# Sums of weight blocks of the two Gates and of two token-row projections on VectorE in place of POOL

## The chip, the cores and the metric

The kernel runs on one core of one Trainium2 chip. The time is that of one launch on the device, in microseconds (us). The core's engines are TensorE (PE: matmuls; PEld: the loading of their stationary operand, which goes beside them), VectorE (DVE), ScalarE (ACT), GpSimd (POOL) and SyncE (SP), on whose queue the kernel's DMAs are issued. Each engine runs its own instructions in the order of the program and waits on semaphores for the others. All data is float32.

## The reference

One layer of a backbone over 1024 latent tokens of width 1024, with 256 context tokens:

```python
def ffn_sublayer(h, shift, scale, gate, g, w_in, w_out):      # w_in 1024 x 5632, w_out 2816 x 1024
    hn = modulate(rmsnorm(h, g), shift, scale)
    a, b = jnp.split(hn @ w_in, 2, axis=-1)
    y = (jax.nn.silu(a) * b) @ w_out
    return h + 0.5 * gate[:, None, :] * y

h  = ffn_sublayer(h, mods[0], mods[1], mods[2], g_ffn1, w_ffn1_in, w_ffn1_out)
hc = ffn_sublayer(hc, mods_c[0], mods_c[1], mods_c[2], g_ffn1, w_ffn1_in, w_ffn1_out)
p_lat = project(h, mods[3], mods[4], g_mix, w_in, PROJ_SIZES)
p_ctx = project(hc, mods_c[3], mods_c[4], g_mix, w_in, ctx_sizes)
...
y_lat = merge_branches(p_lat[4:], hlf + hlb, g_head, g_sgu, w_s, b_s, w_branch_a, w_branch_b, w_out)
h = h + mods[5][:, None, :] * y_lat
h = ffn_sublayer(h, mods[6], mods[7], mods[8], g_ffn2, w_ffn2_in, w_ffn2_out)
return rmsnorm(h, g_final)
```

In place of the dots stand a bidirectional mLSTM over chunks of 128 tokens, fed with q, k, v and gates out of the projection, and a spatial gating unit, fed with two more parts of it (u and vs). `mods` are nine vectors, silu(c) @ w_ada + b_ada.

## The kernel before, in words

**Products.** Every float32 product is made as three matmuls of a rounded type: each operand is split into a high part (a ScalarE cast, L143) and a low part (a VectorE subtraction, L144), and high x high, high x low and low x high are added up in PSUM. L143 and L144 are those two lines of the helper `split`; its results are called `ring` (weights), `fa`, `fb`, `fc`, `mx` (activations) or `fhl` (results that go on to the next product).

**Seven in place of eight.** The big products are cut into 2 x 2 blocks and made with seven block products in place of eight (`p` = 1 to 7). For this, sums and differences of the blocks of the weights are needed, each an operation over 128 x 512 numbers, and sums of the activations (`Factors`, L292), made once. What this case is about is which engine makes the sums of the weights.

**Gate** is the first half of an FFN on the latent tokens: A (Gate 1, weights `w1i`) and B (Gate 2, `w2i`). A has 22 feature blocks f. Each takes seven steps, one for a p, of 12 matmuls with 512 columns (L389), in the order 1, 2, 5, 6, 7, 4, 3 for the first three blocks, the heads, whose steps go side by side, and then woven block by block with the last two steps of a block among the next one's (`self.steps`). Steps 1, 6, 7 and 4 add into one PSUM bank (`qa`), 5 and 3 into a second and 2 into a third (both `qb`). ScalarE copies the result of step 1 (L404) out of the bank before step 6 may write into it, then that of 6 (L410) and 5 (L413); VectorE adds the result of 2 (L406) and 7 (L415), multiplies with that of 4 (L417), adds that of 3 (L420) and multiplies the two halves (L422), after ScalarE's silu (L407, L421). L438 makes sums of the finished blocks for the next product.

`Gate.load` takes a step's weights, splits them into a page of the ring and is called by `fill`, as soon as a page is free. A block has two raw pages of 128 x 1024 (`half`, loaded from L348: a1 a2 and b1 b2, in tiles `rawq`, or `rawh` for the heads). `presum` makes s1 = b1 + b2 (L355) and b1 = a1 - b1 (L356); step 6 makes a1 = s1 - a1 (L371); step 3 makes a2 = a2 - a1 (L373). Four per block, two Gates: 176 sums. The heads' pages are loaded ahead by `preload`, with their presum: for A in the loop of the context's FFN (L921), for B in `fin_o`, while the product with w_o runs. The ring has 4 pages, and 3 (A) or 5 (B) more once the space for them is free.

**Rows** (L1117) makes the projections to v (`wv`) and vs (`wvs`) with the tokens as rows. It too has seven products; its sums are at L1140, L1142, L1144 and L1146, four times each in each projection: 32. `Stream.fill` calls `load` four entries ahead or more. **Pair** makes the other projections; its sums (L1203 to L1207) are on VectorE in both kernels.

**Order.** A scheduler puts the instructions of each engine in order by the dependences of the program as it is written, and each engine then runs them strictly in that order. Beside the Gate of stage A the adaLN vectors are made in the background: `tick` runs a step of them after each step of the Gate (VectorE L749 and L751 over pages `adapg`, 144 loads of 256 KB). Other side work lies in the list `todo`, from which `pump` takes some after each group of matmuls. `Norm` makes the statistics of a norm (TensorE L201, VectorE L210, TensorE L214 `rb`) and writes the normed activations.

Of the kernel before, what the change touches and what calls it, by code (L numbers as in the profile page):

```python
# [13 lines left out]
ALU = mybir.AluOpType  # L14
# [34 lines left out]
def build(tc, a, out):  # L49
    nc = tc.nc  # L50
    ctx = ExitStack()
    with ctx:
        _build(ctx, tc, nc, a, out)


def _build(ctx, tc, nc, a, out):
    V, S, G, T = nc.vector, nc.scalar, nc.gpsimd, nc.tensor
# [38 lines left out]
    def t2(name, dt=F32, shape=(128, 512)):  # L96
        return tp.tile(list(shape), dt, name=name, tag="t2", bufs=12)

    def mm_ps(name):
        return ps.tile([128, 512], F32, name=name, tag="mm", bufs=4)  # L100
# [4 lines left out]
    class Weights:  # L105
# [10 lines left out]
        def load(self):  # L116
            n, i, w = self.order.popleft()
            src = a[n][i]
            if self.n % 4 < 2:
                raw = self.pool.tile([128, w], F32, name="raw", tag="raw", bufs=2)  # L120
            else:
                raw = hnp.tile([128, w], F32, name="raw", tag="pg1", bufs=8)
            self.n += 1
            nc.sync.dma_start(raw, src)
            hl = self.pool.tile([128, 2, w], F32R, name="hl", tag="hl", bufs=3)
            split(hl, raw)
            self.ready.append((n, i, hl))
            self.held += 1
# [13 lines left out]
    def split(hl, src):  # L142
        S.copy(hl[:, 0, :], src)  # L143
        V.tensor_sub(hl[:, 1, :], src, hl[:, 0, :].bitcast(F32))  # L144
# [31 lines left out]
    def proj(pt, wl, pgs, first):  # L176
        mm3(pt, [wk(wl, k) + (pgs[k][:, 0, :], pgs[k][:, 1, :]) for k in range(NKT)], first)
# [138 lines left out]
    class Gate:  # L316
# [31 lines left out]
                nc.sync.dma_start(s[i], a[self.name][2 * f + i])  # L348
            return s[i][:, 0:512], s[i][:, 512:1024]

        def presum(self, f):
            a1, a2 = self.half(f, 0)
            b1, b2 = self.half(f, 1)
            s1 = self.s[f]["s1"] = self.sums("s1")
            G.tensor_tensor(s1, b1, b2, ALU.add)  # L355
            G.tensor_tensor(b1, a1, b1, ALU.subtract)  # L356

        def load(self):
            f, p = key = self.order.popleft()
            if p in (1, 2):  # L360
                src = self.half(f, 0)[p - 1]
                self.half(f, 1)
            else:
                a1, a2 = self.half(f, 0)
                b1, b2 = self.half(f, 1)
                s = self.s[f]

                if p in (5, 6) and "s1" not in s:
                    self.presum(f)
                if p == 6:  # L370
                    G.tensor_tensor(a1, s["s1"], a1, ALU.subtract)  # L371
                elif p == 3:
                    G.tensor_tensor(a2, a2, a1, ALU.subtract)  # L373
                src = {6: a1, 5: s["s1"], 7: b1, 4: b2, 3: a2}[p]
            hl = self.ring()
            split(hl, src)
            self.ready.append((key, hl))
            self.held += 1
            if p == 3:
                del self.s[f]  # L380
# [178 lines left out]
    class Stage:  # L559
# [15 lines left out]
                          lambda n: s1v.popleft(), NFP, HEAD)  # L575
            self.heads = [(f, i) for i in (0, 1) for f in self.q.head]

        def preload(self):
            if self.heads:
                f, i = self.heads.pop(0)  # L580
                self.q.half(f, i)
                if i:
                    self.q.presum(f)

        def rpage(self, name, shape=(128, 2, 512), dt=F32R):
            return self.rg.tile(list(shape), dt, name=name, tag="ring2", bufs=self.ring2)
# [256 lines left out]
    A = Stage("1", "w1i", 3)  # L843
# [53 lines left out]
    def slow(fn, *args, cost=1024):  # L897
        f = it(fn, *args)
        f.cost = cost
        todo.append(f)  # L900

    for f in range(NF):
        if f < NKT:
            for tb in range(2):
                nc.sync.dma_start(h[tb][f], a["xT"][f, :, tb * 512:(tb + 1) * 512])
        if 2 <= f < 2 + NKT:
            for tb in range(2):
                slow(add_pos, tb, f - 2)
                slow(n1[tb].sq, f - 2)
                slow(nc.sync.dma_start, hsp[tb, f - 2], h[tb][f - 2], cost=0)  # L910
        if f == 2 + NKT:
            todo.extend([n1[0].rstd, nop, n1[1].rstd, nop, n1[0].bcast, n1[1].bcast])
            for d in range(NKT):
                slow(n1[0].inplace, d, s0, b0)
                slow(A.F.early, fpage, 1 if d < 4 else 2, d % 4)
            for d in range(NKT):
                slow(n1[1].inplace, d, s0, b0)
        if f == 12:
            A.head()
        if f > 12:  # L920
            A.preload()  # L921
        wa = W.take("w1i", 2 * f)
        wb = W.take("w1i", 2 * f + 1)
        if f % 2 == 0:
            pa, pb = mm_ps("pa"), mm_ps("pb")
        for pt, w_ in ((pa, wa), (pb, wb)):
            proj(pt[:, f % 2 * 256:f % 2 * 256 + 256], w_, hnc, f % 2 == 0)
            W.done()
        if f % 2 == 0:
            continue  # L930
        sil = t2("sil")
        S.activation(sil, pa, AF.Silu)
        V.tensor_mul(sil, sil, pb)
        g = [t2("gc", F32R) for _ in range(2)]
        S.copy(g[0], sil)
        V.tensor_sub(g[1], sil, g[0].bitcast(F32))
        for y in range(2):
            nc.sync.dma_start(gcsp[f // 2, y].rearrange("p f c -> p (f c)"), g[y].bitcast(F32))
# [125 lines left out]
    class Stream:  # L1064
# [13 lines left out]
        def fill(self):  # L1078
            while self.q and len(self.ready) < 4 + self.extra:
                if isinstance(self.q[0], Bar):  # L1080
                    if not self.q[0].up:
                        return
                    self.q.popleft()
                    continue
                load, run = self.q.popleft()
                src = load()
                hl = self.ring()
                split(hl, src)
                self.ready.append((run, hl))
# [27 lines left out]
    class Rows:  # L1117
# [13 lines left out]
        def load(self, p, k):  # L1131
            if p in (1, 2):
                i = k if p == 1 else k + 4
                if i not in self.r:
                    self.get(i, rawpg if p == 1 else raw2)
                return self.r[i][:, 0:512]
            a1, b1 = self.r[k][:, 0:512], self.r[k][:, 512:1024]
            a2, b2 = self.r[k + 4][:, 0:512], self.r[k + 4][:, 512:1024]
            if p == 7:
                G.tensor_tensor(b1, a1, b1, ALU.subtract)  # L1140
            elif p == 6:
                G.tensor_tensor(b2, b2, b1, ALU.subtract)  # L1142
            elif p == 5:
                G.tensor_tensor(a1, a1, b2, ALU.add)  # L1144
            elif p == 3:
                G.tensor_tensor(a2, a2, b2, ALU.subtract)  # L1146
            return {7: b1, 4: b2, 6: b2, 5: a1, 3: a2}[p]

        def prod(self, p, k, hl):
# [112 lines left out]
    def rows_steps(name, emit, side=(), early=False):  # L1262
        r = Rows(name, emit, early)
        n = 0
        for p in RSEQ:
            for k in range(4):
                st.q.append((lambda p=p, k=k: r.load(p, k), lambda hl, p=p, k=k: r.prod(p, k, hl)))
                n += 1
                if n == 4:
                    st.q.append(r.bar)  # L1270
            if p == 2:
                for load, run in side:
                    st.q.append((lambda load=load: load(r), run))
                    n += 1
        return n, r.bar
# [818 lines left out]
```

## Time and profile before

Three runs took 2684.61, 2685.7 and 2685.88 us; the profiled execution took 2682.41 us, with a span of 2680.3 us and a mean granted TensorE clock of 0.997. Its busy times by stage, in us, all from windows of the trace (the moved sums of POOL are in the stages named in bold):

| us from the start | stage | length | PE | DVE | ACT | POOL |
|---|---|---|---|---|---|---|
| 0 to 178 | adaLN, context FFN in | 178 | 171.72 | 132.28 | 97.86 | 12.35 |
| 178 to 603 | **Gate 1** | 425 | 421.46 | 324.88 | 179.38 | 129.82 |
| 603 to 880 | FFN 1 out | 277 | 276.47 | 231.01 | 135.71 | 0.00 |
| 880 to 1060 | **rows of wv**, gates | 180 | 179.18 | 104.10 | 80.72 | 26.93 |
| 1060 to 1380 | projections to q, k, o and more | 320 | 320.00 | 231.42 | 164.71 | 0.00 |
| 1380 to 1560 | **rows of wvs**, context states | 180 | 180.00 | 117.53 | 71.03 | 22.84 |
| 1560 to 1920 | mLSTM heads, w_b | 360 | 357.95 | 247.95 | 85.00 | 115.61 |
| 1920 to 2022 | w_a to w_o, **heads of Gate 2** | 102 | 100.91 | 72.52 | 51.01 | 14.02 |
| 2022 to 2452 | **Gate 2** | 430 | 424.00 | 307.28 | 189.24 | 114.80 |
| 2452 to 2680 | FFN 2 out, final norm | 228 | 218.47 | 147.77 | 87.08 | 4.21 |

How to read the profile: a row of instructions starts with its place in time, or with the line of the kernel; "out<-in" names the tiles; "x24" counts instructions. A wait in square brackets is the engine's idle time ahead of the row and what ended it. In the list of waits, a row is the waiting engine and line, what it waited for, and then the us in total, the number of waits and the longest. An engine's busy time counts overlapping records once. Records of instructions in a row overlap by some 0.08 us, so that two of 0.69 us appear as one row of some 1.3 us.

### The profile page before, as it was taken

Reading aid. Unit: us, or ns where it says so; the run is one execution under the profiler, and the core shown is the slowest. Engines: PE = TensorE matmul, PEld = TensorE weight load, DVE = VectorE, ACT = ScalarE, POOL = GpSimd, SP = SyncE. Lnnn points to the kernel's source line nnn. Section 1 sums busy time; section 2 is a strip of 40 time slices with the busy share of each in tenths; the row PEclk is TensorE's granted clock in tenths of the full one; section 3 lists DMA queues with packets and bytes.
Section 4 is the critical chain, followed back from the end, with each engine's and each line's share of the span. In section 5 each row is a group of like instructions: output and inputs, shape, how many; then the busy total and the mean of one; then the engine's idle time right before and its main releaser. Section 6 shows DMA issues by size and latency. Waiting matters only on the chain.

```text
span 2680.3 us, 35678 instructions
## 1 busy us (share of the span) xinstructions
PE 2650.2 (99%) x12754; PEld 2210.3 (82%) x12754; DVE 1916.7 (72%) x3243; ACT 1141.7 (43%) x1952; POOL 440.6 (16%) x422
## 2 busy tenths in 40 slices
PE   9999999999999999999999999999999999999998
PEld 5998888888889878888888888888887788888887
DVE  4897688686979646687664868677568766675855
ACT  4664444344336525564443443121245444344432
POOL 0041333220000210000002005342102323230000
PEclk9999999999999999999999999999999999999999
DMA  8842344369578222356553467448140332337645
GB/s 299 315 173 99 142 165 149 114 217 327 156 254 281 85 79 86 106 169 199 194 176 105 140 238 268 166 167 279 58 159 24 126 140 99 135 122 274 201 157 173
DMA packets 202240, 456.73 MB, mean 170 GB/s; under 512 B 20432, under 2 KB 54480, under 8 KB 202064
## 3 DMA queue, kind: packets, MB, share of 16 engines
q1 hardware_dynamic: 202064, 454.47, 49.6%
q8 instruction: 100, 1.64, 0.3%
q14 instruction: 76, 0.62, 0.1%
HBM read 328.95 MB, written 125.51 MB: 170 GB/s over the span
## 4 chain that ended last, share of the span: by engine, by line
PE 89%; DVE 6%; issue 2%; DMA 1%; ACT 1%; SPq 0%; POOL 0%; POOLq 0%; ACTq 0%; DVEq 0%
PE pq L1240 17%; PE qa L389 17%; PE po L508 14%; PE qb L389 12%; PE pt L1719 9%; PE pr L1159 6%; PE pc L1030 2%; PE pn L1832 2%; PE pu L1559 2%; PE pa L169 1%; PE pb L169 1%; PE pkc L1219 1%; PE adr L811 1%; PE pn L1830 1%; DVE h L292 1%
## 5 line engine op out<-in xcount | busy, mean ns | idle before, releaser
L144 DVE TENSOR_TENSOR ring<-rawq,ring 128x512 fp32r<-128x512 f32 x408 | 310.6, 762 | 204.9 <-ACT ring L143 202.2
L508 PE MATMUL po<-gring,wring 128*128 128x512 f32 (+1 forms) x1896 | 425.1, 385 | 0.5 <-DMA gring<-fsp 0.5
L508 PEld LDWEIGHTS po<-gring,wring 128*128 128x128 f32 x1896 | 349.5, 188 | 71.9 <-issue 1.0
L143 ACT CAST ring<-rawq 128x512 fp32r<-128x512 f32 x408 | 252.9, 621 | 299.5 <-PE pq L1240 82.1
L389 PE MATMUL qa<-fc,ring 128*128 128x512 f32 x1056 | 252.6, 390 | 2.3 <-DVE ring L144 1.4
L389 PEld LDWEIGHTS qa<-fc,ring 128*128 128x128 f32 x1056 | 198.1, 188 | 44.2 <-DVE ring L144 1.8
L1240 PE MATMUL pq<-fc,ring 128*128 128x512 f32 x864 | 207.8, 393 | 0.0
L143 ACT CAST wring<-rw 128x512 fp32r<-128x512 f32 x154 | 95.9, 622 | 228.3 <-PE po L508 220.9
L1240 PEld LDWEIGHTS pq<-fc,ring 128*128 128x128 f32 x864 | 161.6, 188 | 33.3
L1719 PE MATMUL pt<-yp,ring 128*128 128x512 f32 x768 | 183.9, 396 | 1.2 <-ACT ug L1297 1.2
L144 DVE TENSOR_TENSOR wring<-rw,wring 128x512 fp32r<-128x512 f32 x154 | 106.3, 691 | 93.9 <-ACT wring L143 93.7
L1719 PEld LDWEIGHTS pt<-yp,ring 128*128 128x128 f32 x768 | 144.2, 188 | 30.7 <-ACT ug L1297 1.4
L1240 PE MATMUL pq<-fa,ring 128*128 128x512 f32 x576 | 142.3, 395 | 0.0
L1240 PE MATMUL pq<-fb,ring 128*128 128x512 f32 x576 | 138.2, 394 | 0.0
L389 PE MATMUL qa<-fb,ring 128*128 128x512 f32 x528 | 128.6, 394 | 3.7 <-ACT p L404 3.7
L389 PE MATMUL qa<-fa,ring 128*128 128x512 f32 x528 | 127.7, 391 | 1.2 <-DVE ring L144 0.7
L389 PE MATMUL qb<-fb,ring 128*128 128x512 f32 x528 | 126.8, 390 | 1.2 <-DVE p L406 0.6
L1240 PEld LDWEIGHTS pq<-fb,ring 128*128 128x128 f32 x576 | 107.7, 188 | 23.7 <-issue 0.2
L389 PE MATMUL qb<-fa,ring 128*128 128x512 f32 x528 | 126.2, 389 | 0.0
L389 PE MATMUL qb<-fc,ring 128*128 128x512 f32 x528 | 126.2, 389 | 0.0
L751 DVE SCALAR_TENSOR_TENSOR adacc<-adapg,sc,adacc 128x512 f32<-128x512 f32 x140 | 111.4, 814 | 20.1 <-DMA adapg<-in_w_ada_dram 19.3
L1240 PEld LDWEIGHTS pq<-fa,ring 128*128 128x128 f32 x576 | 106.9, 188 | 22.5 <-DVE ring L144 0.2
(342 smaller groups left out, 4803.9 us busy)
## 6 DMA issues: line engine op xcount, KB each, us to landing
adapg<-in_w_ada_dram SPq DMA_DIRECT2D x144, 256.0 KB, 3.7
fsp<-fhl SPq DMA_DIRECT2D x66, 512.0 KB, 2.6
gring<-fsp SPq DMA_DIRECT2D x66, 512.0 KB, 4.2
raw<-in_w1i_dram SPq DMA_DIRECT2D x44, 512.0 KB, 5.5
graw<-fsp SPq DMA_DIRECT2D x88, 256.0 KB, 3.6
rawq<-in_w1i_dram SPq DMA_DIRECT2D x38, 512.0 KB, 3.4
rawq<-in_w2i_dram SPq DMA_DIRECT2D x38, 512.0 KB, 3.6
fsp<-p SPq DMA_DIRECT2D x66, 256.0 KB, 2.1
```

What stands on the lines that cost most here:

```text
L143: S.copy(hl[:, 0, :], src)
L144: V.tensor_sub(hl[:, 1, :], src, hl[:, 0, :].bitcast(F32))
L169: T.matmul(pt, x, y, start=first and i == 0, stop=i == n - 1, skip_group_check=True)
L389: T.matmul(pt, hl[:, x, sl], pages[p][k][:, y, :], start=first and i == 0, stop=i == 11, skip_group_check=not first)
L508: T.matmul(pt[:, cs], w[:, x, sl], g[:, y, cs], start=grp and kp == 0 and i == 0, stop=kp == NFP - 1 and i == 2, skip_group_check=not grp)
L751: eng.scalar_tensor_tensor(acc, pgt, sc2[:, q, k:k + 1], acc, ALU.mult, ALU.add)
L1030: T.matmul(pt, hl[d // 4][:, x, sl], g[:, y, :], start=f == 0 and d % 2 == 0 and i == 0, stop=f == NF - 1 and i == 2, skip_group_check=True)
L1159: T.matmul(self.pt[m], pg[:, x, sl], hl[:, y, :], start=first and k == 0 and i == 0, stop=k == 3 and i == 2, skip_group_check=not first)
L1240: T.matmul(pt, hl[:, x, k * 128:(k + 1) * 128], pg[k][:, y, :], start=first and k == 0 and i == 0, stop=k == 3 and i == 2, skip_group_chec ...
L1559: T.matmul(pu[:, 0:257], ksl[:, kt * 128:(kt + 1) * 128], wv, start=True, stop=True)
L1719: T.matmul(pt, hl[:, x, k * 128:(k + 1) * 128], pg[:, y, :], start=kh + k + i == 0, stop=kh == 1 and k == 3 and i == 2)
L1832: T.matmul(pn[:, 0:257], qi[:, c_, :], self.C[d][:, c_, :], start=False, stop=c_ == 1)
```

## The change

The four sums of a Gate's block and the four of a Rows entry are issued on VectorE (`V`) in place of POOL (`G`). `presum` and `preload` get an argument for the engine, and only the heads of stage A pass POOL: their six sums at L355 and L356 stay there, while those at L371 and L373 move. No line number changes.

```diff
-        def presum(self, f):
+        def presum(self, f, eng=V):
...
-            G.tensor_tensor(s1, b1, b2, ALU.add)
-            G.tensor_tensor(b1, a1, b1, ALU.subtract)
+            eng.tensor_tensor(s1, b1, b2, ALU.add)
+            eng.tensor_tensor(b1, a1, b1, ALU.subtract)
...
                 if p == 6:
-                    G.tensor_tensor(a1, s["s1"], a1, ALU.subtract)
+                    V.tensor_tensor(a1, s["s1"], a1, ALU.subtract)
                 elif p == 3:
-                    G.tensor_tensor(a2, a2, a1, ALU.subtract)
+                    V.tensor_tensor(a2, a2, a1, ALU.subtract)
...
-        def preload(self):
+        def preload(self, eng=V):
             if self.heads:
                 f, i = self.heads.pop(0)
                 self.q.half(f, i)
                 if i:
-                    self.q.presum(f)
+                    self.q.presum(f, eng)
...
         if f > 12:
-            A.preload()
+            A.preload(G)
...
             if p == 7:
-                G.tensor_tensor(b1, a1, b1, ALU.subtract)
+                V.tensor_tensor(b1, a1, b1, ALU.subtract)
             elif p == 6:
-                G.tensor_tensor(b2, b2, b1, ALU.subtract)
+                V.tensor_tensor(b2, b2, b1, ALU.subtract)
             elif p == 5:
-                G.tensor_tensor(a1, a1, b2, ALU.add)
+                V.tensor_tensor(a1, a1, b2, ALU.add)
             elif p == 3:
-                G.tensor_tensor(a2, a2, b2, ALU.subtract)
+                V.tensor_tensor(a2, a2, b2, ALU.subtract)
```

The scheduler's order moves with it. VectorE, after Gate 1's heads, where the woven blocks begin (about 229 us in the trace before); `s_2417` is the s1 of a block, `u`, `y` and `p` are results of steps, and a row with "x2" stands for two instructions:

```order
 L144 TENSOR_TENSOR fc<-h,fc 128x512
+L355 TENSOR_TENSOR s_2417<-rawq 128x512
 L417 TENSOR_TENSOR p_2072<-p_2072,qa 128x512
-L144 TENSOR_TENSOR ring<-rawq,ring 128x512 x2
-L144 TENSOR_TENSOR ring<-s_2471,ring 128x512
+L144 TENSOR_TENSOR ring<-rawq,ring 128x512
+L356 TENSOR_TENSOR rawq<-rawq 128x512
 L144 TENSOR_TENSOR ring<-rawq,ring 128x512
 L420 TENSOR_TENSOR u_2252<-u_2252,qb 128x512
 L144 TENSOR_TENSOR ring<-rawq,ring 128x512
-L749 TENSOR_SCALAR adacc<-adapg,sc_96 128x512
+L371 TENSOR_TENSOR rawq<-s_2417,rawq 128x512
```

Three sums (L355, L356, L371) now stand in VectorE's queue among the additions that empty PSUM banks, and the splits of the ring come fewer at a time.

VectorE, in the product with w_o, where the pages of Gate 2's heads arrive (`rawh`) and `rawt` are w_o's weights:

```order
 L1962 SCALAR_TENSOR_TENSOR h<-pt,mods,h 128x512
-L144 TENSOR_TENSOR ring<-rawt,ring 128x512 x2
+L144 TENSOR_TENSOR ring<-rawt,ring 128x512
+L356 TENSOR_TENSOR rawh<-rawh 128x512
+L355 TENSOR_TENSOR s1s<-rawh 128x512 x2
+L356 TENSOR_TENSOR rawh<-rawh 128x512
+L144 TENSOR_TENSOR ring<-rawt,ring 128x512
+L356 TENSOR_TENSOR rawh<-rawh 128x512
 L1962 SCALAR_TENSOR_TENSOR h<-pt,mods,h 128x512
```

The heads' sums stand between two splits of w_o's ring.

ScalarE, in the opening of Gate 2 (about 2085 to 2094 us in the trace before); `u_18071` is the second result of the second head, `p_17811` the first of the first, and L404 copies step 1 of the first woven block:

```order
 L421 ACTIVATE u_18071<-u_18071 128x512
+L143 CAST ring<-s_18234 128x512
 L143 CAST fhl<-u_18071 128x512
-L143 CAST ring<-s_18234 128x512
+L143 CAST ring<-rawq 128x512
+L404 COPY p_18315<-qa 128x512
 L143 CAST fhl<-p_17811 128x512
 L421 ACTIVATE u_18100<-u_18100 128x512
-L143 CAST ring<-rawq 128x512
-L404 COPY p_18315<-qa 128x512
```

The copy of L404 moves ahead of the cast of `p_17811` and of a silu; one split of s moves ahead of the cast of `u_18071`. TensorE's order is the same but for the opening of Gate 2, where the statistics' sums (L201) come after 13 matmuls of a step in place of 10, and L214 after 14 in place of 12.

## The prediction

> **What bounds the kernel now.** I read the page's busy times first, then TensorE's waits (all of them, then by stage), then the stages themselves. Below, the first two rows are the page's; the next are TensorE's waits, as line, what it waited for, us in total, times, longest: five in the opening of Gate 2 (2022 to 2094 us), two from Gate 1 (178 to 603), one from the first token-row projection (880 to 950) and one from the seam before w_o (1920 to 2022). The last three are stages: length, then busy us of PE, PEld, DVE, ACT and POOL, with the granted clock behind them.
>
> ```profile
> span 2680.3 us, 35678 instructions
> PE 2650.2 (99%) x12754; PEld 2210.3 (82%) x12754; DVE 1916.7 (72%) x3243; ACT 1141.7 (43%) x1952; POOL 440.6 (16%) x422
> ...
> PE qa L389 <- ACT p L404: 2.3, 1, 2.3
> PE qa L389 <- DVE ring L144: 1.4, 1, 1.4
> PE rb L214 <- DVE diag L210: 1.1, 1, 1.1
> PE qb L389 <- DVE p L406: 0.6, 1, 0.6
> PE qb L389 <- DVE fb L144: 0.5, 1, 0.5
> ...
> PE qa L389 <- ACT p L404: 1.4, 1, 1.4
> PE qa L389 <- DVE y L415: 0.9, 1, 0.9
> ...
> PE pvc L1318 <- DVE nt L225: 0.8, 1, 0.8
> ...
> PE pt L1719 <- DVE mx L144: 0.9, 1, 0.9
> ...
> 244.00:603.00 359.00, 357.79 (x1578) 296.09 (x1579) 278.74 (x386) 146.72 (x254) 106.60 (x69) 1.00 0.46 161
> 2022.00:2094.00 72.00, 66.00 (x286) 52.37 (x285) 67.30 (x100) 43.85 (x78) 16.36 (x10) 1.00 0.06 23
> 2094.00:2452.00 358.00, 358.00 (x1574) 296.29 (x1573) 239.98 (x295) 145.39 (x252) 98.44 (x69) 1.00 0.39 140
> ```
>
> TensorE is the bound: 2650.2 of 2680.3 us busy at full granted clock. The change takes no matmul away, so it can only gain from TensorE's 30 idle us, and only from those near the moved instructions. That is small: the body of Gate 2 has no wait at all (358.00 of 358.00), Gate 1's has 1.2 us. What is left stands where a stage opens. In the opening of Gate 2 VectorE is busy for 67.3 of 72 us, and TensorE waits there for VectorE, or for ScalarE that VectorE holds up. So the question is whether VectorE gets through sooner or later once it makes the sums itself.
>
> **What the change moves.** Gates: 22 blocks by four sums by two Gates are 176, less the 6 of the first Gate's heads at L355 and L356: 170. Rows: 8 by four are 32. So 202 instructions go from POOL to VectorE. No DMA is issued by them; the loads that fill the buffers keep their count, and the order on SP shifts only by a few places. What do they cost? These are groups of equal instructions (count | busy us, mean ns of one | idle before): four on POOL, then the same operation in the same form on VectorE, then VectorE's own work.
>
> ```profile
> L356 POOL TENSOR_TENSOR rawq<-rawq 128x512 f32<-128x512 f32 x38 | 61.7, 1626 | 2.7
> L355 POOL TENSOR_TENSOR s<-rawq 128x512 f32<-128x512 f32 x38 | 56.6, 1491 | 26.3 <-ACT ring L143 22.8 <-DMA rawq<-in_w1i_dram 2.4 <-DMA rawq<-in_w2i_dram 0.9
> L371 POOL TENSOR_TENSOR rawq<-s,rawq 128x512 f32<-128x512 f32 x38 | 56.3, 1483 | 121.4 <-DVE ring L144 105.6 <-issue 15.8
> L373 POOL TENSOR_TENSOR rawq<-rawq 128x512 f32<-128x512 f32 x38 | 54.9, 1444 | 401.4 <-DVE ring L144 401.4
> ...
> L1204 DVE TENSOR_TENSOR rawq<-rawq 128x512 f32<-128x512 f32 x24 | 16.5, 686 | 0.5
> ...
> L422 DVE TENSOR_TENSOR u<-u,y 128x512 f32<-128x512 f32 x44 | 48.7, 1108 | 1.5 <-ACT u L421 0.7
> L420 DVE TENSOR_TENSOR u<-u,qb 128x512 f32<-128x512 f32 x44 | 30.1, 684 | 26.3 <-PE qb L389 26.3
> L144 DVE TENSOR_TENSOR fhl<-p,fhl 128x512 fp32r<-128x512 f32 x22 | 31.5, 1431 | 0.0
> L144 DVE TENSOR_TENSOR fhl<-u,fhl 128x512 fp32r<-128x512 f32 x22 | 15.1, 685 | 0.0
> L144 DVE TENSOR_TENSOR ring<-s,ring 128x512 fp32r<-128x512 f32 x62 | 54.3, 876 | 28.9 <-ACT ring L143 28.8
> L144 DVE TENSOR_TENSOR ring<-rawq,ring 128x512 fp32r<-128x512 f32 x408 | 310.6, 762 | 204.9 <-ACT ring L143 202.2
> ```
>
> A sum takes 1444 to 1626 ns on POOL and 686 on VectorE. So the added work is 202 x 0.686 = 139 us. Against it stands what VectorE's rows show of POOL: the two fhl groups are the same instruction, but one takes 685 ns and the other 1431. Single rows of the opening show when:
>
> ```profile
> 2060.01 1.78 DVE L144 TENSOR_TENSOR ring<-rawh,ring 128x512 fp32r<-128x512 f32 x1
> 2061.72 3.47 DVE L144 TENSOR_TENSOR fc<-h,fc 128x512 fp32r<-128x512 f32 x2
> ...
> 2080.83 1.78 DVE L144 TENSOR_TENSOR ring<-s,ring 128x512 fp32r<-128x512 f32 x1
> 2082.54 1.78 DVE L144 TENSOR_TENSOR ring<-rawq,ring 128x512 fp32r<-128x512 f32 x1
> ...
> 2086.04 1.77 DVE L422 TENSOR_TENSOR u<-u,y 128x512 f32<-128x512 f32 x1
> ...
> 2061.21 3.44 POOL L356 TENSOR_TENSOR rawq<-rawq 128x512 f32<-128x512 f32 x2
> 2080.45 3.32 POOL L371 TENSOR_TENSOR rawq<-s,rawq 128x512 f32<-128x512 f32 x2 [15.80 <-issue]
> ```
>
> The columns are start, us, engine, line and operation. VectorE's instructions last 1.7 to 1.8 us each while POOL sums (2086.04 lies beside a sum of L373), and 0.69 otherwise: each POOL sum stretches one VectorE instruction by about 1.1 us, if one of this kind is there. L420, which has one operand in PSUM, keeps its 684 ns. Over four groups the excess is 44 x 0.424 + 22 x 0.746 + 62 x 0.187 + 408 x 0.073 = 18.7 + 16.4 + 11.6 + 29.8 = **76.5 us** over the 685 that such an instruction takes undisturbed. So VectorE gains 139 us of work and loses at least 77 of stretching: busy time 1917 + 139 - 77 = 1979 at most; smaller groups not shown are stretched as well, and I expect about **1940 us** (1915 to 1980). POOL keeps 440.6 less the moved 202 x 1.5 = 303: about 138 us.
>
> **In the bodies of the Gates: nothing.** The 69 sums of POOL in each body become 69 x 0.686 = 47 us on VectorE: 278.7 + 47 = 326 of 359 us in Gate 1 even if no stretching went, 287 of 358 in Gate 2. TensorE is full there; the cover is the ring of split weights, which VectorE fills ahead. If that cover were gone, every microsecond would count; that is the slow rival. In-order queueing is the new wait: a sum that waits for its load now holds back every VectorE instruction behind it, among them L415, L417 and L420 that free PSUM banks. The loads have landed some steps ahead (the idle of 2.4 and 0.9 us behind DMA over 38 sums at L355 is what POOL ever waited), so I take 0 of a possible 0 to 3.3 us lost, nearest to the Gate 2 row, and keep 3 for the range.
>
> **At the openings: the gain.** Its largest piece is the wait for L404 in Gate 2. These are TensorE's rows around it, ScalarE's ahead of it, and VectorE's ahead of Gate 1's 0.9:
>
> ```profile
> 2088.53 2.88 PE L389 MATMUL qb<-fa,ring 128*128 128x512 f32 x12
> 2093.70 4.61 PE L389 MATMUL qa<-fb,ring 128*128 128x512 f32 x12 [2.29 <-ACT p L404]
> ...
> 2090.47 0.62 ACT L143 CAST fhl<-u 128x512 fp32r<-128x512 f32 x1 [1.40 <-DVE u L422]
> ...
> 2093.08 0.57 ACT L404 COPY p<-qa 128x512 f32<-128x512 f32 x1
> ...
> 370.95 1.78 DVE L751 SCALAR_TENSOR_TENSOR adacc<-adapg,sc,adacc 128x512 f32<-128x512 f32 x1
> ```
>
> ScalarE sat idle for 1.40 us before 2090.47, waiting for L422, which VectorE made late after the stretched rows above; then four more instructions stood between that cast and L404's copy, and they fill the 2.6 us from one start to the other at some 0.52 each. In the new order only one stands between them (the ring cast of s goes ahead, into the idle 1.40 us; the fhl cast of p and the silu go behind the copy), so it starts 3 x 0.52 = 1.6 us earlier, and sooner still if VectorE is not stretched. I take 1.8 of the 2.3. Behind the wait, 12 matmuls take 4.61 us where the 12 ahead took 2.88: 1.7 us more, paid only because TensorE had stood; if the wait falls to half a microsecond I take that as gone. From the other four: 1.2 of the 1.4 (L144 for the ring, late by the stretched pair at 2061.72), 0.5 of 1.1 (the diagonal; TensorE has two more matmuls ahead of L214 in the new order), 0.4 of 0.5 (fb), and 0.6 of 0.6 (L406). Sum of the opening: 1.8 + 1.7 + 1.2 + 0.5 + 0.4 + 0.6 = **6.2 us**.
>
> One rule bears on the 1.7. The Trainium skill, "TensorE: Matmul & The Clock Gate", Part 1: The HAM clock gate, says that the array falls to half rate after at least one idle window of about 3.4 us. The trace shows a slow group behind a wait of 2.29 us, so here row and rule differ; by the rule alone this group would owe nothing to the wait and the sum would be 1.7 us smaller. The measurement decides.
>
> The other openings: Gate 1's L404 wait has the same picture (a pair at L371 on POOL beside two stretched ring rows), 1.4 of 1.4. L415's 0.9 at 372 lies behind the stretched 370.95 row; in its place a sum stands in the queue, so I take 0 of 0.9. Seam: the heads' sums of Gate 2 ran on POOL beside the splits of mx and now come later, between w_o's ring splits; 0.9 of 0.9. Row projection: 0.5 of 0.8. Sum: 6.2 + 1.4 + 0 + 0.9 + 0.5 = **9.0 us**. Both ends: 0 if each wait comes back elsewhere; at most all nine waits, 9.9, with the 1.7 behind the longest about 12.
>
> The profiled execution took 2682.41 us, 2.1 more than its span and 3.3 less than the median of 2685.7. Its 9.0 us carried to the median: 2685.7 - 9.0 = **2676.7**.
>
> **Rivals.** *No change that can be measured* (0.2%, 5.4 us, is about what a measurement of this kernel can tell from none): the work VectorE gains replaces stretching one for one, and in the opening, where VectorE is busy for 67 of 72 us, the ten sums add 10 x 0.686 = 6.9 us against 6.5 us of stretch removed (the rows above: six instructions, 1.78 + 3.47 + 1.78 + 1.78 + 1.77 = 10.6 us, less 6 x 0.69). Then a wait for L404 turns into one for L144 or L415. It would give 0 to 5 us of gain: about 2683. For it speaks the full VectorE; against it, ScalarE's new order, which does not rest on VectorE's speed. The Trainium skill speaks for it too: "Perfetto Trace Analysis", Optimizing Scalar/DVE Operations, says that GpSimd and VectorE share an SBUF read port, so moving work between those two might not help; the stretched rows agree that they share something.
>
> *Slower*: VectorE becomes the bound in the body of Gate 1, where the adaLN background also runs on it. There it waits as follows:
>
> ```profile
> DVE ring L144 <- ACT ring L143: 46.0, 28, 2.5
> DVE adacc L751 <- DMA adapg<-in_w_ada_dram: 6.4, 5, 1.7
> ```
>
> Gate 1's body holds 19 blocks of 84 matmuls (1578 in its row), 359 / 19 = 18.9 us each. VectorE has 278.7 / 19 = 14.7 of work and 52.4 / 19 = 2.8 of these waits per block; 47 / 19 = 2.5 more makes 20.0. So if no stretching goes, it needs 1.1 us per block more than TensorE gives: 19 x 1.1 = 21, less the 6.2 of Gate 2: 2685.7 + 15 = **2701**. It decides from 18.9 us on. Against it: the stretching does go with POOL's sums, by 76.5 x 69 / 202 = 26 us or 1.4 per block, which leaves 18.6, and the waits for ScalarE are partly waits of an engine that is early.
>
> *It does not do what it says*: excluded, since the new order has 202 more instructions on VectorE. *All waits go*: 2674, inside the forecast's own range.
>
> **How the numbers follow.** Forecast, 2672.5 (12 less, and 1.2 for the spread of the runs of before) to 2680.3: 0.64. No measurable change, 2680.3 to 2691.1: 0.27. Slower, beyond: 0.09. The range takes the forecast whole and most of the second case, with the 3 us of sums that wait for loads on top of its 2685: 2672.5 to 2688. Faster 0.64, same 0.27, slower 0.09.
>
> **What would show it.** Right: no VectorE row of 1.7 us beside sums, L422 and fhl<-p at about 690 ns, VectorE's busy time near 1940, POOL's near 138; in Gate 2's opening a wait for L404 below 0.6 us and 12 matmuls behind it in 2.9; PE waits of the bodies still about 0. Wrong: a new wait of TensorE for L144, L415 or L420 in the bodies, or idle time of VectorE behind loads at L355; then the time stays at 2683 or goes up. A wait for L404 that stays with undisturbed VectorE rows would mean that ScalarE's order sets it.

## The result, and the profile after

| | median us | runs | lowest to highest |
|---|---|---|---|
| before | 2685.79 | 4 | 2684.61 to 2686.82 |
| changed | 2669.86 | 4 | 2669.07 to 2671.69 |

The changed kernel is 15.9 us faster, ratio 0.9942 with a 95% interval of 0.9925 to 0.9959 (11 to 20 us). The forecast was 9 us. The profiled executions stand 13.5 us apart (spans 2680.3 and 2666.8). In two later sessions the changed kernel's medians were 2672.01 and 2672.07, and those of before 2686.08 and 2684.9: a gain of 13 to 14 us.

The first two rows are the page of the changed kernel; then the four stages of its windows (length, busy us of PE, PEld, DVE, ACT and POOL, granted clock, DMA share, GB/s), and all that is left in its list of waits for the stretch 178 to 603.

```profile
span 2666.8 us, 35493 instructions
PE 2643.5 (99%) x12754; PEld 2207.5 (83%) x12754; DVE 1918.6 (72%) x3445; ACT 1142.6 (43%) x1952; POOL 136.4 (5%) x220
...
178.00:244.00 66.00, 65.29 (x288) 53.69 (x288) 46.26 (x74) 32.96 (x57) 0.00 (x0) 1.00 0.18 63
244.00:603.00 359.00, 359.00 (x1587) 297.29 (x1586) 284.83 (x459) 146.87 (x254) 0.00 (x0) 1.00 0.46 163
2022.00:2094.00 72.00, 72.00 (x317) 59.17 (x317) 69.69 (x121) 47.15 (x84) 0.00 (x0) 1.00 0.13 48
2094.00:2452.00 358.00, 358.00 (x1581) 296.45 (x1580) 231.81 (x365) 148.04 (x257) 0.00 (x0) 1.00 0.40 144
...
PE qa L389 <- DVE ring L144: 0.7, 1, 0.7
```

In the opening of Gate 2 TensorE is now busy for 72.00 of 72 us, against 66.00 before. All the waits that the prediction quoted are gone; the 0.7 us that is left, at 179 us, lies ahead of the moved sums. VectorE does 202 instructions more in about the same busy time, 1918.6 against 1916.7 us. Its groups show why (count | busy us, mean ns of one | idle before):

```profile
L144 DVE TENSOR_TENSOR ring<-rawq,ring 128x512 fp32r<-128x512 f32 x408 | 280.9, 690 | 222.2 <-ACT ring L143 218.8 <-DMA ybsp<-mx 2.0
L144 DVE TENSOR_TENSOR ring<-s,ring 128x512 fp32r<-128x512 f32 x62 | 42.6, 688 | 25.9 <-ACT ring L143 25.8
L422 DVE TENSOR_TENSOR u<-u,y 128x512 f32<-128x512 f32 x44 | 30.2, 687 | 0.6
L355 DVE TENSOR_TENSOR s<-rawq 128x512 f32<-128x512 f32 x38 | 26.0, 684 | 1.0 <-DMA rawq<-in_w1i_dram 1.0
L144 DVE TENSOR_TENSOR fhl<-p,fhl 128x512 fp32r<-128x512 f32 x22 | 15.0, 684 | 0.0
```

A sum costs 684 ns, and the instructions that lasted 762, 876, 1108 and 1431 ns on average now all last 684 to 690.

The largest wait shows how the gain adds up. These are TensorE's rows around L404 in Gate 2: first before (the row that followed the two shown with the prediction), then the same steps of the changed kernel, then ScalarE's there.

```profile
2098.15 2.90 PE L389 MATMUL qb<-fb,ring 128*128 128x512 f32 x12
```
```profile
2079.67 2.88 PE L389 MATMUL qb<-fa,ring 128*128 128x512 f32 x12
2082.39 2.88 PE L389 MATMUL qa<-fb,ring 128*128 128x512 f32 x12
2085.11 2.88 PE L389 MATMUL qb<-fb,ring 128*128 128x512 f32 x12
```
```profile
2079.19 0.62 ACT L143 CAST fhl<-u 128x512 fp32r<-128x512 f32 x1 [1.42 <-DVE u L422]
2079.92 0.62 ACT L143 CAST ring<-rawq 128x512 fp32r<-128x512 f32 x1
2080.45 0.58 ACT L404 COPY p<-qa 128x512 f32<-128x512 f32 x1
```

From the start of step 2 (`qb<-fa`) to that of the step behind the next took 2098.15 - 2088.53 = 9.62 us before and takes 5.44 now: a wait whose row says 2.29 us cost 4.18.

The same was done for every wait that the prediction named, and for one of 0.2 us at the seam, with the starts of the same 28 matmuls in both traces (14 ahead of the wait and 14 behind it; 30 at the diagonal). Undisturbed, 28 take 6.35 us. The last column is a kernel told of below.

| wait | its row, us | lost before | lost, changed | lost, fills for sums (E6) |
|---|---|---|---|---|
| Gate 1, L404 | 1.4 | 1.73 | 0 | 0 |
| Gate 1, L415 | 0.9 | 1.24 | 0 | 0 |
| rows, nt L225 | 0.8 | 1.06 | 0.06 | 0 |
| seam, mx | 0.9 | 1.18 | 0 | 0 |
| seam, ring | 0.2 | 0.49 | 0 | 0 |
| Gate 2, diagonal L210 | 1.1 | 1.65 more than the changed kernel | 0 | 1.23 more |
| Gate 2, fb | 0.5 | 0.84 | 0 | 0 |
| Gate 2, L406 | 0.6 | 0.98 | 0 | 0 |
| Gate 2, ring | 1.4 | 1.75 | 0 | 0 |
| Gate 2, L404 | 2.3 | 4.19 | 0 | 0 |
| sum | 10.1 | 15.1 | 0.1 | 1.2 |

15.1 us at these places, between the 13.5 of the profiled pair and the 15.9 of the medians. The rest of the two traces drifts by 1 to 2 us either way at places that the change doesn't touch: before is 1.9 us longer in the first 20 us (the adaLN loads) and 1.3 us shorter at 1700 to 1800 us. Runs of one kernel drift as well: the spans of three profiled runs of the changed kernel are 2666.8, 2667.0 and 2671.5 us.

### The profile page after: what moved, and what is told of

It reads as the page before. It is cut to its first block, busy times and chain, and to the rows that moved or that the text cites. A ratio compares the mean times of both kernels' runs of the same rounds, so it can differ in the third digit from the quotient of the medians.

```text
span 2666.8 us, 35493 instructions
## 1 busy us (share of the span) xinstructions
PE 2643.5 (99%) x12754; PEld 2207.5 (83%) x12754; DVE 1918.6 (72%) x3445; ACT 1142.6 (43%) x1952; POOL 136.4 (5%) x220
## 4 chain that ended last, share of the span: by engine, by line
PE 91%; DVE 4%; DMA 2%; issue 2%; ACT 0%; SPq 0%; POOL 0%; POOLq 0%; ACTq 0%; DVEq 0%
PE qa L389 18%; PE pq L1240 17%; PE po L508 14%; PE qb L389 13%; PE pt L1719 9%; PE pr L1159 6%; PE pc L1030 2%; PE pn L1832 1%; PE pu L1559 1%; PE pa L169 1%; PE pb L169 1%; PE pkc L1219 1%; PE pvc L1318 1%; PE adr L811 1%; PE pn L1830 1%
## 5 line engine op out<-in xcount | busy, mean ns | idle before, releaser
L144 DVE TENSOR_TENSOR ring<-rawq,ring 128x512 fp32r<-128x512 f32 x408 | 280.9, 690 | 222.2 <-ACT ring L143 218.8
L144 DVE TENSOR_TENSOR wring<-rw,wring 128x512 fp32r<-128x512 f32 x154 | 106.0, 688 | 95.7 <-ACT wring L143 95.5
L143 ACT CAST ring<-rawt 128x512 fp32r<-128x512 f32 x64 | 39.7, 620 | 189.0 <-PE pt L1719 179.8
```

## The experiments

Each was timed beside the kernel before, 5 to 11 runs of each; E1 to E4 in one session, E5 to E8 in a second, E9 to E11 in a third. The theory: POOL's sums stretch VectorE's instructions, and that makes the openings late. The rivals: the scheduler's new order did it, or the way through POOL (a longer sum, two handovers more) was late.

**E1. The stretch brought back, all orders kept.** In Gate 2, each sum on VectorE is followed by an addition on POOL that nobody waits for:

```diff
+        echo = lambda q, x: q.name == "w2i" and G.tensor_tensor(cst[:, 1:5].rearrange("p a b -> p (a b)"), x, x, ALU.add)
...
-            eng.tensor_tensor(s1, b1, b2, ALU.add)
+            eng.tensor_tensor(s1, b1, b2, ALU.add); self.echo(s1)
```

and so behind the other three sums.

> The changed kernel, and for each of the 88 sums of Gate 2 one more addition on POOL (the result added to itself, into constants that are dead by then and that nobody reads). The orders of TensorE, VectorE, ScalarE and SyncE are those of the changed kernel, instruction by instruction, and nothing waits for the additions but the release of pages. Theory (the gain of Gate 2's opening came from POOL no longer stretching VectorE): VectorE's rows of 1.7 to 1.8 us return in Gate 2, and so do TensorE's waits in 2022 to 2094 us, at least the 5.9 us of before since VectorE now makes the sums as well; with the slow matmuls behind them 6 to 15 us more than the changed kernel, 2676 to 2685. Rival 1 (the new order of ScalarE and VectorE made the gain): the opening stays without waits, 2669 to 2671. Rival 2 (the way through POOL, a longer sum and two more handovers ahead of a split, was what came late): also 2669 to 2671, since no split waits for POOL.

Measured: 2676.96 us (2670.43 to 2679.74), ratio to before 0.9968 (0.9956 to 0.998): about 5 to 7 us of the gain given back by the median, though one of the five runs, at 2670.43, lies where the rivals put it. The rows of the opening: TensorE's waits in 2024 to 2100 us, its row behind L404, and VectorE's rows beside POOL's additions.

```profile
PE qa L389 <- ACT p L404: 1.6, 1, 1.6
PE rb L214 <- DVE diag L210: 0.5, 1, 0.5
...
2091.84 3.06 PE L389 MATMUL qa<-fb,ring 128*128 128x512 f32 x12 [1.62 <-ACT p L404]
...
2085.95 1.52 DVE L356 TENSOR_TENSOR rawq<-rawq 128x512 f32<-128x512 f32 x1
2087.40 2.12 DVE L144 TENSOR_TENSOR ring<-s,ring 128x512 fp32r<-128x512 f32 x2
...
2085.56 1.37 POOL L318 TENSOR_TENSOR cst<-s 128x512 f32<-128x512 f32 x1
```

L404's wait is back at 1.6 us with ScalarE's order unchanged from the changed kernel, so that order alone doesn't remove it: both rivals miss this. But only 2.1 of the 5.9 us of waits came back, fewer than the theory asked for. Priced as in the table they cost 2.6 us (1.95 at L404, 0.7 at the diagonal); the rest of what this profiled run is longer stands far from Gate 2, at places where other runs differ as well (1.6 us at 950 to 1060 us, 3.4 at 1560 to 1600). So of the 5 to 7 us of the median, only these 2.6 are shown to come from the stretching. POOL's additions read one tile, take 1.04 to 1.37 us in the opening, and the VectorE rows beside them that are stretched take 0.9 to 1.5 us, not 1.8. And they follow the sums, which VectorE makes after 2070 us, while POOL had made them at 2059 to 2064, where L144 for the ring was late. So E1 shows that stretching makes L404 late, and tests the other waits only in part.

**E2, E3, E4. One part of the change each.** Gate 2 alone, Gate 1 alone, the Rows alone, each with the other sums left on POOL:

```diff
+        eng = property(lambda self: V if self.name == "w2i" else G)
...
-        def presum(self, f):
+        def presum(self, f, eng=None):
+            eng = eng or self.eng; a1, a2 = self.half(f, 0)
```

(for E3 with `"w1i"`; E4 has the eight changed lines of `Rows.load` and no other).

> Only the sums of Gate 2 (its heads too) go to VectorE; Gate 1 and the Rows stay as before. By the alignment of the two traces, the seam gave 1.7 us and Gate 2's opening 9.6: 11.3 us, 2674.5. Rival: part of that is run to run scatter (the profiled run of before was 3.3 us faster than its median), and the whole 15.9 us of the medians is spread over all parts: then 2676 to 2680.

> Only the sums of Gate 1 (but those of its heads at L355 and L356) go to VectorE. The traces gave 1.7 us at its start and 1.2 at the wait for L415: 2.9 us, 2682.9. Rival (VectorE near its limit in Gate 1, hidden by what the other parts gain): no gain or a loss, 2685 to 2690.

> Only the 32 sums of the two token-row projections go to VectorE. One wait of 0.8 us at 908 us goes, 1.0 us in the aligned traces: 2684.7, which the runs can hardly tell from before. Rival: the 1.4 us that the changed kernel lost in the mLSTM heads (waits of 0.6 and 0.8 us for VectorE at L1835 and L1836) come from the Rows' new order; then those two waits stand here too and the time is 2685 to 2687.

| | median us | ratio to before, 95% interval | us below 2685.74 |
|---|---|---|---|
| E2, Gate 2 | 2675.0 | 0.9959 (0.9947 to 0.9971) | 10.7 |
| E3, Gate 1 | 2681.57 | 0.9983 (0.9975 to 0.9992) | 4.2 |
| E4, Rows | 2684.21 | 0.9995 (0.9987 to 1.0004) | 1.5 |

They add up to 16.4 us, and each part's waits are gone in its own trace and stand in the other two (at the seam in another row, with the same loss). E3's gain is clear of no change, so Gate 1 has no hidden loss; E4's is not, and only its trace shows the wait at L225 gone. The waits at L1835 and L1836 in the changed kernel's mLSTM stage don't come from the Rows: E2 and E3, without the Rows' change, have 0.9 and 1.0 us of them too, and the profiled run of before has none, so they vary from run to run.

E3 and E4 hold one thing more. Both still have L404's wait of Gate 2; here are the rows behind it, first E3's, then E4's:

```profile
2092.58 3.03 PE L389 MATMUL qa<-fb,ring 128*128 128x512 f32 x12 [2.33 <-ACT p L404]
```
```profile
2099.26 4.61 PE L389 MATMUL qa<-fb,ring 128*128 128x512 f32 x12 [2.31 <-ACT p L404]
```

The same wait was followed by slow matmuls in E4 and in the profiled run of before, not in E3. The 1.7 us are thus not a fixed part of the price.

**E5, E11. The changed kernel again.**

> The changed kernel once more, in the session in which the next ones run. The four runs of it so far lie within 2.6 us (2669.07 to 2671.69) while other kernels of this study scatter by 8 to 10 us, so its median is uncertain by some us. Summing the pieces that came back in the runs with one part each (10.7 + 4.2 + 1.5 = 16.4 us): 2669.3. By the aligned traces' pieces at the changed places alone (11.3 + 3.0 + 1.0 = 15.3): 2670.4. If the profiled pair (13.5 us) is the truth: 2672.

> The changed kernel for the comparison with the two above: 2669 to 2672.

Measured: 2672.01 us (ratio 0.9947, 0.9935 to 0.996) and 2672.07 (0.9949, 0.9936 to 0.9962). The first median was 2 us low; against before in the same sessions the gains are 14.1 and 12.8 us, so the sum of the single parts, 16.4, overstates, and the places' 15.1 and the pair's 13.5 are nearer.

**E6. Old order, POOL kept in the chain, but without reading.** The kernel before, each sum of weights on POOL replaced by two fills of its tile; the sums are left out:

```diff
-            G.tensor_tensor(s1, b1, b2, ALU.add)
+            G.memset(s1, 0.5); G.memset(s1, 0.25)
```

> The kernel before, with each of POOL's 202 sums and the six of Gate 1's heads replaced by two fills of the same tile, so POOL writes but reads nothing; the sums of weights are left out. TensorE's order is that of the kernel before, ScalarE's and VectorE's too but for some neighbours that change places, and the splits still wait for POOL. Theory (POOL's reading of SBUF stretches VectorE, and that makes the openings late): no VectorE row of 1.7 us in the Gates, the waits of the openings go, L404's included, and the time falls by 10 to 16 us, 2670 to 2676. Rival 1 (the new order made the gain): the waits stay, 2683 to 2686. Rival 2 (the way through POOL is late): a fill is shorter than a sum, so the waits behind splits of sums (L144 ring) shrink, those for L210, fb and L415 stay: 2680 to 2684.

Measured: 2668.13 us (2666.23 to 2671.16), ratio 0.994 (0.9927 to 0.9954), 18 us below before and 2 below the range expected; 2.0 us of that lie at 140 to 190 us, where the heads of Gate 1 are summed (E7). First its page's busy times; then one of POOL's groups, two of VectorE's, and the only wait in the opening.

```profile
PE 2644.9 (99%) x12754; PEld 2209.0 (83%) x12754; DVE 1800.4 (68%) x3243; ACT 1144.8 (43%) x1952; POOL 341.0 (13%) x630
...
L355 POOL MEMSET s<- 128x512 f32 x76 | 40.0, 531 | 80.1 <-DVE ring L144 55.3 <-DVE h L292 22.8
...
L422 DVE TENSOR_TENSOR u<-u,y 128x512 f32<-128x512 f32 x44 | 30.4, 691 | 1.6 <-ACT u L421 0.7
L144 DVE TENSOR_TENSOR fhl<-p,fhl 128x512 fp32r<-128x512 f32 x22 | 15.0, 682 | 0.0
...
PE rb L214 <- DVE diag L210: 0.6, 1, 0.6
```

This decides between the theory and both rivals in Gate 2, where TensorE's and ScalarE's orders are those of before, the splits still wait for POOL, and two fills keep it busy for about 1.1 us per sum. Yet no VectorE row of 128x512 in the Gates is stretched and every wait but one is gone. VectorE's order in Gate 2 is that of before but for 2082 to 2098 us: there some neighbours change places, and one split of the ring fewer stands ahead of the L422 that ScalarE waits for, which accounts for 0.6 us. The three rows that were stretched there, by 1.1 us each, account for 3.3, more than the whole wait for L404. And ScalarE still sits idle there for POOL, 1.31 us for the fill of L373 against 1.72 for the sum before, so the way through POOL didn't make L404 late. Where Gate 1's woven blocks begin (about 228 to 268 us), VectorE's and ScalarE's orders both differ, so for L404's wait in Gate 1 this run doesn't separate stretching from order.

At the ten places, 15.1 - 1.2 = 13.9 us come back (last column of the table). The exception is the diagonal, where 0.6 us of 1.1 stay. Here are its four rows of L210 in before, in E6 and in the changed kernel:

```profile
2026.95 1.89 DVE L210 TENSOR_SCALAR diag<-cst,rs_y 128x128 f32<-128x128 f32 x4
```
```profile
2019.01 1.43 DVE L210 TENSOR_SCALAR diag<-cst,rs_y 128x128 f32<-128x128 f32 x4
```
```profile
2023.91 0.88 DVE L210 TENSOR_SCALAR diag<-cst,rs_y 128x128 f32<-128x128 f32 x4
```

Undisturbed, one lasts 0.28 us. In before, one takes 1.30 beside a sum of L373; in E6, three take 0.50 to 0.63 beside the fills of L373. So this instruction is stretched by fills too, by 0.55 us in all, which is most of the wait that stays: E6 doesn't show that the new order (two more matmuls ahead of L214) was needed for it. The fills are shorter than the sums (1.1 against 1.5 us), so a part of the chain got shorter too; but the waits for L210, fb, L406 and L415 have no split of a sum behind them, and three of these four are gone as well.

It also sizes the stretching: VectorE falls from 1916.7 to 1800.4 us, 116 us in all for the 208 sums that no longer read.

**E7, E10. The heads of Gate 1 on VectorE as well.**

```diff
-            A.preload(G)
+            A.preload()
```

> The changed kernel with the six sums of Gate 1's heads (L355, L356 in the loop of the context's FFN) on VectorE as well. Theory: six stretched rows less, six sums of 0.686 more, and TensorE waits there for VectorE's splits of hl (1 to 2 us in all, not at one place in two runs): -1 to +1 us against the changed kernel, not to be told from it. Rival (VectorE is tight there, which is why these stayed): waits for hl grow, +2 to +5 us.

> The kernel with Gate 1's heads on VectorE too, against the changed kernel on one chip. The first time it stood 3.6 us below the changed kernel's median of that session, but scatter of such medians is 2 to 3 us, and of the difference of the traces about 1 us lies where the heads are summed. If it is real: 1 to 3 us below; if scatter: within 1 us.

Measured: 2668.41 us (2665.79 to 2671.73) beside 2672.01 of E5, and 2668.06 (2665.76 to 2670.11) beside 2672.07 of E11: 3.6 and 4.0 us below the changed kernel, more than either expectation had. TensorE's waits in 130 to 190 us, in the profiled run of the changed kernel and then in E10's (E7's list has 0.6 us behind L144's ring as well):

```profile
PE pa L169 <- DVE hl L144: 0.9, 1, 0.9
PE qa L389 <- DVE ring L144: 0.7, 1, 0.7
PE qa L389 <- ACT ring L143: 0.5, 1, 0.5
PE pb L169 <- DVE hl L144: 0.4, 1, 0.4
```
```profile
PE qa L389 <- ACT ring L143: 0.5, 1, 0.5
```

The same 352 matmuls between 140 and 190 us take 47.83 us in E10, 48.68 in E7, 48.01 in E6, and 49.95 to 50.67 in the ten other profiled runs. In the changed kernel's trace three sums of activations (L292) last 1.78 us there, beside POOL's sums of the heads. So 1.3 us (E7 against E5) and 2.5 us (E10 against E11) of the 3.6 and 4.0 are seen where these sums lie; the rest isn't placed. Of the versions that compute the whole result this one has the lowest medians.

**E8. POOL's products of L1826 on VectorE too.**

```diff
-                        G.tensor_tensor(qi[:, c_, :], self.qT[c_][:, n * 128:(n + 1) * 128],
+                        V.tensor_tensor(qi[:, c_, :], self.qT[c_][:, n * 128:(n + 1) * 128],
```

> The changed kernel with POOL's 128 products of L1826 (128x128, 63 us on POOL, beside the mLSTM heads) on VectorE too. If POOL's reading stretches VectorE everywhere, this stage gains as well; but TensorE's waits there are only 3.3 us, of which 1.4 stand behind VectorE's L1835 and L1836 and 0.8 behind L1854, so at most 2 us less than the changed kernel. Rival: the products stand in the chain from TensorE's step to the next (each waits for pn), and behind VectorE's queue they come later than on POOL, which had nothing else to do: 2 to 10 us more.

Measured: 2670.94 us (2669.91 to 2673.82) beside 2672.01 of E5: not to be told apart. The waits at L1835, L1836 and L1854 (2.2 us) left its list, and nothing came late behind VectorE's queue, so the rival is out. The 1.1 us between the medians is within their scatter and less than those waits were; that it comes from them is not shown, since the waits at L1835 and L1836 vary from run to run.

**E9. Each sum of L355 five times over.** In the woven blocks, four more sums per block on VectorE:

```diff
-            eng.tensor_tensor(s1, b1, b2, ALU.add)
+            for _ in range(n): eng.tensor_tensor(s1, b1, b2, ALU.add)
```

> The changed kernel, with the sum of L355 made five times over in each of the 19 woven blocks of both Gates: 152 sums more on VectorE, 4 x 0.60 = 2.4 us per block, the result unchanged. It asks whether the bodies of the Gates have room on VectorE, as the prediction took it. Theory: VectorE has about 285 of 359 us of work in Gate 1's body and 232 of 358 in Gate 2's; 46 us more make 331 and 278, so both bodies keep TensorE full (waits of under 1 us in all); the openings, where VectorE is busy for 70 of 72 us, pay for the first blocks' extra sums: 2 to 6 us in all, 2672 to 2677. Rival (the slow case of the prediction: work and waits for ScalarE and DMA together pass 18.9 us a block in Gate 1, 15.0 + 2.6 + 2.4 = 20.0): a wait in most of Gate 1's blocks, 19 x 1.1 = 21 us more, about 2691.

Measured: 2672.79 us (2671.48 to 2675.78) beside 2672.07 of E11. The bodies of the two Gates, length and busy us as above:

```profile
244.00:603.00 359.00, 359.00 (x1587) 297.38 (x1586) 324.06 (x533) 148.29 (x255) 0.00 (x0) 1.00 0.48 163
2094.00:2452.00 358.00, 358.00 (x1581) 296.54 (x1580) 279.42 (x445) 148.59 (x260) 0.00 (x0) 1.00 0.41 145
```

VectorE does 39 and 48 us more, and TensorE still stands still for nothing. The rival's 21 us did not come, and the opening paid next to nothing: its list of waits stayed empty, and the matmuls around L404 lost 0.25 us.

## Why the prediction was right in its direction, and short in size

- **What bounds the kernel**: right. No matmul went, and the gain lies in TensorE's waits at the openings and in the matmuls just behind them. But of the 13.5 us between the two profiled runs the page books 6.7 as busy time (2650.2 to 2643.5) and 6.8 as idle: "only from those near the moved instructions" looked at the idle half alone.
- **VectorE's account**: right, at the edge. It said 1915 to 1980 us and took 1940; 1918.6 was measured. The stretching was right: 1940 leaves 116 us for it, above the 77 counted from four groups (78 if all four are measured from 685 ns), and E6 has 116. Too large was the work: a sum's record takes 686 ns, but records in a row overlap by 0.08 us, so a sum adds about 0.60 us, some 122 for 202 in place of 139. POOL's 138 is 136.4.
- **Nothing in the bodies**: right, but for the wait for L415 in Gate 1 (below). They are full at 359.00 and 358.00, and E9 shows that 39 to 48 us more on VectorE would still be free. The slow rival fell on its sum: it added VectorE's waits for ScalarE and DMA to its work, and those waits are slack.
- **L404's wait and its mechanism**: right; E1 brought the wait back by stretching alone. The part given to ScalarE's new order (1.6 of 1.8 us) was not needed: with ScalarE's old order the wait goes as well (E6).
- **Where it failed: the terms of the sum.** The prediction took 9.0 us, and the same places gave 15.1. It failed twice. First in the shares: it took 7.3 us of waiting of the 10.1 that the rows show (1.8 of 2.3, 0.5 of 1.1, 0.5 of 0.8, and 0 of 0.9 for L415, "in its place a sum stands in the queue"), though the sum there takes 0.68 us where the stretched row took 1.78, and though at the diagonal, where it counted on TensorE's order, a row of L210 took 1.30 us beside a sum in place of 0.28. All ten waits went: 2.8 us more than it took. Second in the price of a wait: it used the idle us of the row. Lost between the starts of the same matmuls were 15.1 us, of which 1.7 in the slow group; the remaining 3.3 us over ten waits are 0.3 us for each, beyond its row. The two make up the 6.1 us between 9.0 and 15.1. The "at most about 12" was therefore no bound, and the range built on it ended at 2672.5, above the medians of 2669.86 to 2672.07.
- **No measurable change** as a rival: wrong on "one for one". VectorE's busy times in the window 2022 to 2094 us, 67.30 before and 69.69 after, hold different work, since the changed kernel is further on by then (317 matmuls of TensorE against 286). While TensorE makes the same 267 matmuls, from the step behind the norm (2025.43 us before, 2021.63 after) to L404's, VectorE is busy for 65.3 us before and 58.4 after, the sums included. What went was more than what came, and it had fallen on urgent instructions: the L422 that ScalarE waited for ended behind three rows of 1.8 us.
- The rule of the Trainium skill that stood beside that rival ("Perfetto Trace Analysis", Optimizing Scalar/DVE Operations: moving work between GpSimd and VectorE might not help) did not apply here: the change made the kernel 13 to 16 us faster. The trace agrees instead with the Trainium skill's "SBUF — State Buffer", Who interferes with whom, which says that a VectorE instruction with two SBUF inputs contends with a GpSimd instruction that reads SBUF, not with one that only writes it: `fhl<-p` took 1431 ns on average in before, where POOL makes sums, and 682 in E6, where it makes fills.

## What to carry to other kernels

Where two engines slow each other down, moving work from the slower to the faster one can shorten the busy engine's queue although it gets more to do (here 202 instructions more in the same busy time); look for one instruction in one form that has two durations. Price a wait by the starts of the instructions on both sides of it in an undisturbed and a disturbed stretch, not by the idle time in its row. A replacement that keeps the order and the handovers but drops the reading (here fills for sums) tells contention from order in one run, where it doesn't stretch anything itself (here it did at L210).

## What the runs showed of the hardware

TensorE loses more than it waits. Behind nine of the ten waits the first matmul starts its successor 0.34 us later in place of 0.227, and the next ones run some ns slow. Behind a standstill of 2.7 us from start to start, 8 matmuls in before and 7 in E4 ran 0.427 us apart and none in E3, with the same wait of 2.3 us ahead. The granted clock shows it: 0.53 at 2096 to 2098 us in before and 0.50 at 2100 to 2102 in E4, against 1.00 at 2096 to 2098 in E3. Behind 2.0 us (E1) no matmul was slow, but behind 2.2 us in E11 (a wait of 1.77 us at L1170) seven were. It also came with no wait at all: in five of the thirteen profiled runs (E1, E2, E4, E8, E11) 6 or 7 matmuls of the gates' stage, near 995 us, ran 0.427 us apart, shortly behind 20 matmuls of 16 columns each (L1425, 2.4 us); the granted clock at 994 to 997 us was 0.50 in E11 and 1.00 in the changed kernel's first profiled run. That is 1.6 us of the scatter between runs. So whether the slow rate is met depends on more than the wait's length. The Trainium skill, "TensorE: Matmul & The Clock Gate", Part 1: The HAM clock gate, calls the window in which activity is counted free-running, which fits one wait with two outcomes; its figure of about 3.4 us of idling does not fit the slow groups behind 2.3.
